# One 32-byte tile fewer ahead of two large operands: a float32r encoder trunk on one core

## The chip, the cores and the metric

The kernel runs on one core of a Trainium2 chip. The metric is the time of one execution on the device in microseconds. Before the change the median of 3 runs is 942.32 us (942.11 to 942.88).

## The reference

Two layers of a bidirectional encoder on x of 256 tokens by 1024 features, float32. Each layer is a half-weighted SwiGLU feed-forward part (FFN), a mixer, and a second FFN part, each behind an RMS norm and added to x. The mixer of layer 0 (even) runs a gated MLP over chunks of 128 tokens beside a differential attention, that of layer 1 (odd) a latent attention beside a grouped attention with axial rotary angles.

```python
for l in range(DEPTH):                                   # 2 layers
    x = x + 0.5 * swiglu(rmsnorm(x, ffn1_norm[l]), ffn1_w_gu[l], ffn1_w_down[l])
    h = rmsnorm(x, ...) @ w_in                           # 1024 -> 2560 (even), 1184 (odd)
    x = x + mixer(h) @ w_out                             # 1024 -> 1024
    x = x + 0.5 * swiglu(rmsnorm(x, ffn2_norm[l]), ffn2_w_gu[l], ffn2_w_down[l])
# swiglu(h): g, u = split(h @ w_gu); (silu(g) * u) @ w_down, width 2816
```

## The kernel before

**Precision.** Each float32 matrix is used as a sum of two float32r parts, hi and lo. A product of two such matrices is hi·hi + lo·hi + hi·lo, three products.

**Weights.** They come from HBM in loads of at most 128 x 2048 floats into four `raw` tiles. `fetch` turns each half (1024 columns) into a `hi` tile (copied, mostly by ScalarE) and a `lo` tile (raw minus hi, by VectorE), in rings of six tiles each.

**Activations.** `xs` (128 x 8 x 2 x 256) holds the normed x: for each of 8 slices of 128 features the 256 tokens of the hi part and behind them the 256 of the lo part. `region` (128 x 11264) holds in an FFN its hidden values `hs` (22 x 2 x 256, in the same form), and in a mixer the head outputs `os_` and the queries and keys.

**Four kinds of matmul stream** follow from this. The stationary operand is written first in the code as `lhsT`, the moving one as `rhs`.

- `wide`, in the FFN: one matmul with a hi weight stationary and 512 columns moving (hi and lo of a slice of `xs` or `hs` at once), then one with the lo weight stationary and the 256 hi columns moving. This is called a pair below. Gate and up take 1408 pairs, with `xs` moving; down takes 682 pairs, with `region` moving.
- `dense` in `out_product` and in the last output tile of the last FFN: three matmuls with weights stationary and 256 columns of `region` moving, 150 such triples.
- `dense` in `block` (the projections into the mixers): here a 128-token part of `xs` is stationary and a row of `hi` or `lo` moves: 512 columns (96 triples), 416 columns (16 triples, of the odd projection `c`) or 256 columns (16 triples, of `k`). `small` does the same with parts of `region` stationary, 12 triples.
- `rms_along`: two matmuls with `onesr` stationary and 256 columns of `acc2` moving, once for each FFN.

In a triple all three matmuls add to the same part of a PSUM bank; in a pair the second adds to half of what the first wrote, and the next pair goes to another bank.

**Order of the work.** `Program` records all instructions, plans an order with its own costs, and emits them in that order; all planned instructions appear in the profile under the line of `emit` that calls them, L285. Dependencies go by the name of a tile and the offsets in it.

**Addresses.** `keep` takes a tile from one pool, and the tiles lie one behind the other in each partition, in the order of the calls, each rounded up to a multiple of 32 bytes. In the program as built, `hi0` begins at byte 76928, which is 128 past a multiple of 256; the other `hi` and `lo` tiles follow in steps of 4096, so all begin at 128 past. `gx` begins at 147968, `ident` at 156416, `ones` at 156928 and `onesr` at 157440, all at multiples of 256. Then comes `warm`, one float in a partition, at 157952, a multiple of 256; it takes 32 bytes. So `region` begins at 157984 and `xs` at 203040, both 32 past a multiple of 256; `rr`, `rb`, `acc`, `acc2` and the tables of the mixers follow, with `rb`, `acc` and `acc2` at 64 past. All slices of `xs` and `hs` that a pair uses begin at multiples of 1024 bytes from there. In the block of 416 columns, a row is 1664 bytes, six and a half times 256, so of the two rows in a `hi` or `lo` tile the first begins at 128 past a multiple of 256 and the second at a multiple of 256.

**Turning tiles.** `sm` is a `Turns` object: 32 tiles of 20 floats, and each call gives a view of the next one, in turn. Small sums and factors of the norms and softmaxes lie in them. They are used in turn by their place in the row of calls, so that call n and call n + 32 share a tile.

**`warm`** is written by one ScalarE activation in the preamble (a Silu over one column of `ones`), ahead of all planned work, and read by nothing.

Of the kernel before, what the change touches and what calls it, by code (L numbers as in the profile page):

```python
# [351 lines left out]
def trunk_kernel(ctx: ExitStack, tc: tile.TileContext, a: dict, out: bass.AP):  # L352
# [20 lines left out]
    def keep(nm, *shape, dt=F32):  # L373
        return sb.tile([P, *shape], dt, name=nm)
# [38 lines left out]
    sm = Turns("sm", 32, 20)  # L413
# [32 lines left out]
    nc.vector.memset(ones, 1.0)  # L446
    onesr = keep("onesr", P, dt=F32R)
    nc.vector.tensor_copy(out=onesr, in_=ones)
    warm = keep("warm", 1)
    nc.scalar.activation(out=warm, in_=ones[:, :1], func=AF.Silu)  # L450
    make_identity(nc, ident)
    with lead(90e3):
# [706 lines left out]
```

## Time and profile before

| | |
|---|---|
| median of 3 runs | 942.32 us |
| profiled execution: its time | 942.35 us |
| its span (first to last instruction) | 940.6 us |
| PE busy | 934.3 us, 5564 matmuls |
| VectorE, ScalarE busy | 724.2 us, 548.2 us |
| chain that ended last | PE 97% |

The span is what lies between the first and the last instruction of the profiled execution; the rest of its time lies around it. PE is the matrix engine, PEld its weight load, which runs beside the matmuls. A matmul's own duration reaches past the start of the next one, since they are pipelined: what a stream costs is read from the distance between starts.

### The profile page before, as it was taken

Reading aid. Unit: us, or ns where it says so; the run is one execution under the profiler, and the core shown is the slowest. Engines: PE = TensorE matmul, PEld = TensorE weight load, DVE = VectorE, ACT = ScalarE, POOL = GpSimd, SP = SyncE. Lnnn points to the kernel's source line nnn. Section 1 sums busy time; section 2 is a strip of 40 time slices with the busy share of each in tenths; the row PEclk is TensorE's granted clock in tenths of the full one; section 3 lists DMA queues with packets and bytes.
Section 4 is the critical chain, followed back from the end, with each engine's and each line's share of the span. In section 5 each row is a group of like instructions: output and inputs, shape, how many; then the busy total and the mean of one; then the engine's idle time right before and its main releaser. Section 6 shows DMA issues by size and latency. Waiting matters only on the chain.

```text
span 940.6 us, 14528 instructions
## 1 busy us (share of the span) xinstructions
PE 934.3 (99%) x5564; PEld 825.5 (88%) x5564; DVE 724.2 (77%) x1326; ACT 548.2 (58%) x938; POOL 27.2 (3%) x57
## 2 busy tenths in 40 slices
PE   9999999999999999999999999999999999999998
PEld 8888888888899888888888888888989988888887
DVE  7998786579989878876588887756888698888652
ACT  7765655446856656655465656544587566565530
POOL 0910000000000000000000000000000000000000
PEclk9999999999999999999999999999999999999999
DMA  8774555553365555555555555554412355555530
GB/s 335 260 268 179 185 194 203 180 179 135 102 212 176 184 192 204 186 179 188 202 184 188 185 198 199 180 184 164 181 54 85 105 186 203 179 185 202 199 110 22
DMA packets 26421, 167.83 MB, mean 178 GB/s; under 512 B 2928, under 2 KB 5104, under 8 KB 7024
## 3 DMA queue, kind: packets, MB, share of 16 engines
q1 hardware_dynamic: 26352, 166.92, 50.4%
q8 instruction: 43, 0.70, 0.3%
q14 instruction: 26, 0.21, 0.1%
HBM read 165.86 MB, written 1.05 MB: 177 GB/s over the span
## 4 chain that ended last, share of the span: by engine, by line
PE 97%; DVE 1%; ACT 1%; DMA 0%; issue 0%; SPq 0%; ACTq 0%
PE bank L285 97%; DVE t L285 0%; ACT t L285 0%; DMA raw<-in_gu 0%; DVE sm L285 0%; ACT hi L285 0%; DVE region L285 0%; DVE lo L285 0%; ACT L285 0%; DVE hi L285 0%; DVE ssg L285 0%; DVE gx L285 0%; SPq L285 0%; DVE ssc L285 0%; DVE rc L285 0%
## 5 line engine op out<-in xcount | busy, mean ns | idle before, releaser
L285 DVE TENSOR_TENSOR lo<-raw,hi 128x1024 fp32r<-128x1024 f32 (+2 forms) x318 | 382.6, 1205 | 161.9 <-ACT hi L285 156.4
L285 ACT ACTIVATE hi<-raw 128x1024 fp32r<-128x1024 f32 (+3 forms) x310 | 322.8, 1044 | 301.1 <-PE bank L285 188.9
L285 PE MATMUL bank<-xs,hi 128*128 128x512 f32 x1408 | 490.7, 393 | 0.3 <-ACT hi L285 0.3
L285 PE MATMUL bank<-xs,lo 128*128 128x256 f32 x1408 | 394.9, 280 | 0.0
L285 PEld LDWEIGHTS bank<-xs,hi 128*128 128x128 f32 x1408 | 265.4, 188 | 58.9 <-ACT hi L285 0.6
L285 PE MATMUL bank<-region,hi 128*128 128x512 f32 (+1 forms) x982 | 291.4, 359 | 0.0
L285 PEld LDWEIGHTS bank<-xs,lo 128*128 128x128 f32 x1408 | 265.3, 188 | 0.7 <-DVE lo L285 0.7
L285 PE MATMUL bank<-region,lo 128*128 128x256 f32 x832 | 232.8, 280 | 0.0
L285 PEld LDWEIGHTS bank<-region,hi 128*128 128x128 f32 x982 | 174.0, 188 | 28.4
L285 PEld LDWEIGHTS bank<-region,lo 128*128 128x128 f32 x832 | 156.3, 188 | 0.0
L285 ACT ACTIVATE t<-bank 128x256 f32<-128x256 f32 (+1 forms) x201 | 76.6, 399 | 39.9 <-PE bank L285 38.8
L285 PE MATMUL bank<-hi,xs 128*128 128x512 f32 (+2 forms) x256 | 78.7, 381 | 0.0
L285 DVE TENSOR_TENSOR t<-bank,t 128x256 f32<-128x256 f32 x176 | 67.3, 420 | 0.7 <-ACT t L285 0.7
L285 DVE TENSOR_TENSOR t<-t,rb 128x512 f32<-128x512 f32 x88 | 60.3, 690 | 1.2
L285 PEld LDWEIGHTS bank<-hi,xs 128*128 128x128 f32 x256 | 47.1, 188 | 8.6
L285 DVE SCALAR_TENSOR_TENSOR gx<-bank,gx 128x256 f32<-128x256 f32 (+1 forms) x71 | 28.3, 451 | 27.2 <-PE bank L285 27.2
L285 PE MATMUL bank<-lo,xs 128*128 128x512 f32 (+2 forms) x128 | 48.0, 375 | 0.0
L285 DVE TENSOR_TENSOR t<-t,t 128x256 f32<-128x256 f32 (+2 forms) x108 | 45.9, 429 | 0.1
L285 ACT ACTIVATE t<-t 128x256 f32<-128x256 f32 (+2 forms) x98 | 39.0, 406 | 3.1 <-DVE t L285 3.0
L285 DVE TENSOR_TENSOR region<-t,region 128x256 fp32r<-128x256 f32 (+2 forms) x92 | 39.2, 431 | 1.1 <-ACT region L285 1.1
L285 ACT ACTIVATE region<-t 128x256 fp32r<-128x256 f32 (+1 forms) x89 | 35.6, 405 | 1.4 <-DVE t L285 1.2
L285 ACT ACTIVATE xs<-gx 128x256 fp32r<-128x256 f32 x48 | 24.0, 499 | 10.8 <-DVE gx L285 10.0
(129 smaller groups left out, 466.8 us busy)
## 6 DMA issues: line engine op xcount, KB each, us to landing
raw<-in_gu SPq DMA_DIRECT2D x86, 1024.0 KB, 4.8
raw<-in_dn SPq DMA_DIRECT2D x44, 1024.0 KB, 4.8
raw<-in_ev_in SPq DMA_DIRECT2D x10, 1024.0 KB, 4.9
raw<-in_ev_out SPq DMA_DIRECT2D x4, 1024.0 KB, 5.1
raw<-in_od_out SPq DMA_DIRECT2D x4, 1024.0 KB, 4.9
raw<-in_gu SPq DMA_DIRECT2D x8, 256.0 KB, 4.5
raw<-in_od_q SPq DMA_DIRECT2D x2, 1024.0 KB, 4.8
raw<-in_od_c SPq DMA_DIRECT2D x2, 832.0 KB, 4.4
```

The costliest lines, as they stand in the source:

```text
L285: r = fn(*map(real, args), **{k: real(v) for k, v in kw.items()})
```

## The change

`warm` is no longer a tile of its own. The activation in the preamble writes to the first turning tile instead, and the first call in the planned work gets the second. Everything that lay behind `warm` lies 32 bytes lower: `region` at 157952 and `xs` at 203008, both multiples of 256; `rb`, `acc` and `acc2` go from 64 to 32 past a multiple of 256. What lies ahead of `warm` stays.

```diff
     onesr = keep("onesr", P, dt=F32R)
     nc.vector.tensor_copy(out=onesr, in_=ones)
-    warm = keep("warm", 1)
+    warm = sm(1)
     nc.scalar.activation(out=warm, in_=ones[:, :1], func=AF.Silu)
     make_identity(nc, ident)
```

## Rows read from the trace of the kernel before

**Rows 1.** The page: span, busy time (share) and instructions, chain that ended last.
```profile
span 940.6 us, 14528 instructions
...
PE 934.3 (99%) x5564; PEld 825.5 (88%) x5564; DVE 724.2 (77%) x1326; ACT 548.2 (58%) x938; POOL 27.2 (3%) x57
...
PE 97%; DVE 1%; ACT 1%; DMA 0%; issue 0%; SPq 0%; ACTq 0%
```

**Rows 2.** Waits of PE, the longest: who for whom, us in total, times, longest.
```profile
PE bank L285 <- DVE ones L446: 1.0, 1, 1.0
```

**Rows 3.** Matmuls by shape: out<-operands, shapes, count, busy us, mean ns, idle.
```profile
L285 PE MATMUL bank<-xs,hi 128*128 128x512 f32 x1408 | 490.7, 393 | 0.3 <-ACT hi L285 0.3
...
L285 PE MATMUL bank<-region,hi 128*128 128x512 f32 x682 | 236.6, 392 | 0.0
...
L285 PE MATMUL bank<-region,hi 128*128 128x256 f32 x300 | 54.8, 284 | 0.0
...
L285 PE MATMUL bank<-hi,xs 128*128 128x512 f32 x192 | 63.7, 401 | 0.0
```

**Rows 4.** Timeline of PE in gate and up: start us, us, instruction; first, last.
```profile
59.86 0.39 PE L285 MATMUL bank<-xs,hi 128*128 128x512 f32 x1
...
90.71 0.39 PE L285 MATMUL bank<-xs,hi 128*128 128x512 f32 x1
```

**Rows 5.** Timeline of PE in down, first and last.
```profile
149.99 0.39 PE L285 MATMUL bank<-region,hi 128*128 128x512 f32 x1
...
180.84 0.39 PE L285 MATMUL bank<-region,hi 128*128 128x512 f32 x1
```

**Rows 6.** Stretches: us, busy and count of each engine, PEclk, DMA share, GB/s.
```profile
59.86:90.71 30.85, 30.85 (x180) 27.16 (x179) 25.68 (x43) 18.80 (x34) 0.00 (x0) 1.00 0.59 211
```

**Rows 7.** Timeline of PE in a block of 512 columns, first and last.
```profile
197.54 0.39 PE L285 MATMUL bank<-lo,xs 128*128 128x512 f32 x1
...
204.54 0.39 PE L285 MATMUL bank<-lo,xs 128*128 128x512 f32 x1
```

**Rows 8.** Timeline of PE in the block of 256 columns, first and last.
```profile
665.32 0.28 PE L285 MATMUL bank<-lo,xs 128*128 128x256 f32 x1
...
667.12 0.29 PE L285 MATMUL bank<-lo,xs 128*128 128x256 f32 x1
```

**Rows 9.** Timeline of PE in the block of 416 columns, first and last.
```profile
672.02 0.35 PE L285 MATMUL bank<-lo,xs 128*128 128x416 f32 x1
...
680.60 0.35 PE L285 MATMUL bank<-lo,xs 128*128 128x416 f32 x1
```

**Rows 10.** Timeline of PE in the even out_product, first and last.
```profile
274.91 0.28 PE L285 MATMUL bank<-region,lo 128*128 128x256 f32 x1
...
283.71 0.28 PE L285 MATMUL bank<-region,lo 128*128 128x256 f32 x1
```

**Rows 11.** Timeline of PE in the odd out_product, first and last.
```profile
742.07 0.28 PE L285 MATMUL bank<-region,lo 128*128 128x256 f32 x1
...
751.68 0.28 PE L285 MATMUL bank<-region,lo 128*128 128x256 f32 x1
```

**Rows 12.** Timeline of PE in rms_along: its two matmuls, and the next.
```profile
294.28 0.40 PE L285 MATMUL bank<-acc,onesr 128*128 128x256 f32 x2
...
294.52 0.39 PE L285 MATMUL bank<-xs,hi 128*128 128x512 f32 x1
```

**Rows 13.** Weight loads by shape: weights stationary, then parts of xs.
```profile
L285 PEld LDWEIGHTS bank<-xs,hi 128*128 128x128 f32 x1408 | 265.4, 188 | 58.9 <-ACT hi L285 0.6
...
L285 PEld LDWEIGHTS bank<-hi,xs 128*128 128x128 f32 x256 | 47.1, 188 | 8.6
```

**Rows 14.** VectorE by shape: writes to region, to acc, to t.
```profile
L285 DVE TENSOR_TENSOR region<-t,region 128x256 fp32r<-128x256 f32 x88 | 36.8, 422 | 1.1 <-ACT region L285 1.1
...
L285 DVE TENSOR_TENSOR acc<-acc,t 128x256 f32<-128x256 f32 x42 | 17.7, 423 | 0.2
...
L285 DVE TENSOR_TENSOR t<-t,t 128x256 f32<-128x256 f32 x96 | 40.1, 422 | 0.1
```

## The prediction

> **What bounds the kernel now.** I read the page first. The matrix engine is busy for 934.3 of 940.6 us, and the chain of work that ended last lies on it for 97% [rows 1]. The list of its waits comes next: the longest is 1.0 us, for the first tile at the start [rows 2]. So neither weights nor evictions hold PE up, and VectorE (77%) and ScalarE (58%) work beside it. The end moves only if the matmuls themselves follow each other at another distance.
>
> The groups by shape say where they are [rows 3]: 1408 pairs of gate and up, 682 pairs of down, then the triples. Their mean durations (393 ns for 512 columns) overlap the next matmul, so the distance has to be read from the timeline. In gate and up 89 pairs start between 59.86 and 90.71 us [rows 4]: 30.85 us / 89 = 346.6 ns a pair. In down 89 pairs take 30.85 us too [rows 5], the same 346.6 ns, though another tile moves. The 2090 pairs are 2090 x 0.3466 = 724 us, three quarters of the span. The granted clock is 1.00 in that stretch, the upper level of 2.4 GHz [rows 6]. A pair moves 768 columns; at one column a cycle that is 320 ns. So 26.6 ns a pair (55.6 us over all) is something other than columns, and this is the only thing that an address could change.
>
> **The change part by part.**
>
> *The tile itself.* The activation that writes `warm` stays, ahead of all planned work: 0. The turning tiles shift by one, for all calls alike, so call n still shares its tile with call n + 32 and with no other. The planned dependencies, and with them the order, are the same. One new pair shares a tile: the activation of the preamble and the 32nd call, whose writer comes long after it: 0. If a semaphore had to be looked at there, it would be on VectorE or ScalarE, with 23% and 42% of their time free [rows 1].
>
> *Moving operands of the pairs.* `xs` and `region` go from 32 past a multiple of 256 bytes to 0 past it. No stream in the trace moves float32r columns that always start at 0 past, so I bound it by the neighbours.
> - 128 past, in `block`: ten triples of 512 columns take 204.54 - 197.54 = 7.00 us [rows 7], 233.3 ns a matmul; five triples of 256 take 1.80 us [rows 8], 120.0 ns. One of each would be 353.3 ns, 6.7 more than an FFN pair.
> - Half at 128 past and half at 0 past, in the block of 416 columns: 15 triples take 680.60 - 672.02 = 8.58 us [rows 9], 190.7 ns a matmul. The straight line between the two points above gives 120.0 + 160 x 113.3 / 256 = 190.8 ns for 416 columns. So the half of the matmuls that begins at a multiple of 256 has not made this stream faster or slower than 128 past would.
> - 32 past, in the two output products: 25 triples of 256 columns take 283.71 - 274.91 = 8.80 us [rows 10], 117.3 ns a matmul; 27 triples take 751.68 - 742.07 = 9.61 us [rows 11], 118.6 ns. The two have the same addresses within 256 bytes and still differ by 1.3 ns: a stream can settle at one of several distances without any change of alignment.
> - 64 past, with `onesr` stationary at 0 past: the two matmuls of `rms_along` take 0.24 us [rows 12], 120 ns each, to some 5 ns.
>
> So 256 columns cost 117 to 120 ns from every start that the trace has. The value I take is 0 for the pairs: the nearest row with starts at multiples of 256, that of 416 columns, lies on the line of the others. The bounds stay wide, because that row mixes two starts and has another stationary operand. Upwards: the pair becomes as slow as the block's streams, 2090 x 6.7 ns = +14.0 us. Downwards: the same difference with the other sign, -14.0 us, since no row shows a pair faster than 346.6 ns.
>
> The Trainium skill, page "TensorE: Matmul & The Clock Gate", section "Back-to-back issue gap", has a rule that a matmul of N columns takes N / 2.4 + 2.5 ns at the upper clock. By it a pair is 324.9 ns, 21.7 less than the rows show, and the trace disagrees with it in each of its float32r streams, at four different starts. If the whole of that surplus came from the misplaced start, the change would give 2090 x 21.7 ns = 45 us and a time near 897 us; I hold that for a rival of 2 in 100.
>
> *The 450 matmuls of 256 columns from `region` (150 triples).* 0, with +0.9 us as the bound above (450 x (120.0 - 118.0)), and -0.9 us below. Their distance may also jump between the 117.3 and 118.6 ns already seen, 0.6 us.
>
> *Stationary operands.* In the blocks, parts of `xs` (in `small`, of `region`) are loaded as weights, now from 0 past. The load's own duration is 188 ns there and 188 ns where `hi` is loaded from 128 past [rows 13]. So 0. The bound below: if the start of the stationary operand is why the blocks are slower than the FFN, 288 matmuls of 512 columns get back 233.3 - 229 = 4 ns, 48 of 416 about 3 ns and 48 of 256 about 2 ns: -1.4 us. (The 229 is the pair's 346.6 less the 117.5 of its 256 columns.) Above: +1.4 us, the same size.
>
> *Element-wise work.* VectorE writes 128 x 256 to `region` (32 past) in 422 ns, to `acc` (64 past) in 423 and to `t` (128 past) in 422 [rows 14]: no start costs anything, and there is slack besides. 0.
>
> Sum: 942.35 us of the profiled execution (span 940.6 and 1.75 around it) + 0 = 942.3 us. That execution lies 0.03 us from the median of the three runs, so no correction is needed.
>
> **The rivals.**
>
> *An aligned start makes the moving reads cheaper.* Something in the 26.6 ns surplus depends on whether a row of columns begins inside a block of 256 bytes: 2048 bytes from 32 past touch nine such blocks, from 0 past eight. For it: the surplus is there in every stream, and all streams of one start throughout lie off the multiple. Against: 416 columns, above. Price: up to 6.7 ns a pair, with half of that as the likeliest, 3.3 x 2090 = -7.0 us: 935.3 us; the whole of it gives 928.3. It decides from 0.9 ns a pair on (1.9 us).
>
> *A start at the multiple behaves like 128 past, not like 32 past.* The FFN pairs have the shortest distance that the trace shows, and it could be 32 past that gives it: a row that begins off the larger boundaries may meet the weight load of the next matmul at another place. The place is each of the 2090 pairs, the price up to 6.7 ns: 942.3 + 14.0 + 0.9 = 957.2 us; with half of it 949.3 us. For it: 416 columns, half of them at 0 past, cost as much as the slower line. Against: the blocks differ in more than the start (three matmuls in a row add to one part of a bank, and `xs` is the stationary side), and 256 columns from 64 past cost no more than from 32. It decides from the same 0.9 ns on, upwards.
>
> *The change doesn't do what it says.* It moves only what lies behind `warm`; if the moved addresses leave every stream as it is, only the stationary side of the blocks can answer, within 1.4 us. That is the forecast's own case, and its time could be 941 to 944.
>
> **How the numbers follow.** A measurement of this kernel can tell about 0.2% (1.9 us) from no change. No change within that: 0.47. Aligned reads are cheaper: 0.33, and the surplus gone altogether 0.02, so faster is 0.35. The start at the multiple is worse: 0.18. The predicted time is that of the likeliest case, 942.3 us, whose own range is 940.5 to 944.2. The range for 8 in 10 takes in most of the first rival (down to 931 us, a little above its whole price) and the smaller prices of the second (up to 948 us); outside are the full gain with the skill's surplus (0.07) and the upper half of the loss (0.10).
>
> **What would show it.** If I am right, the starts of the pairs in gate and up and in down still lie 346.6 ns apart, the 512-column block stays near 233 ns, and the span moves by under 2 us. If the first rival holds, both kinds of pairs shorten alike, since both moving tiles shift, while the 512-column block stays. If only the blocks shorten, it was the stationary side. If the second holds, the pairs come near 350 to 353 ns. A change of order on any engine, or a new wait of PE over 1 us, would show that the reasoning on the turning tiles is wrong.

## The result and the profile after

The change makes the kernel slower: 951.55 us (median of 4, 951.31 to 951.72) against 942.60 (median of 4), ratio 1.0094 with a 95% interval of 1.0082 to 1.0105. The prediction was 942.3 us with 931 to 948 for the range, so the time lies outside it.

The page after, span, busy time and the chain that ended last:

```profile
span 949.8 us, 14528 instructions
...
PE 942.0 (99%) x5564; PEld 829.1 (87%) x5564; DVE 725.1 (76%) x1326; ACT 548.5 (58%) x938; POOL 28.1 (3%) x57
...
PE 95%; DVE 2%; DMA 1%; ACT 1%; SPq 0%; issue 0%; ACTq 0%; DVEq 0%
```

Against [rows 1] the span is 9.2 us longer, PE is busy for 7.7 us more, and the instructions are the same in number and, engine by engine, in the same order. PE still hardly waits: its two longest waits (us in total, times, longest) are

```profile
PE bank L285 <- DVE lo L285: 1.3, 3, 0.9
PE bank L285 <- DVE ones L446: 1.1, 1, 1.1
```

The timeline of PE, first in gate and up, then in down, 90 pairs each (start in us, duration):

```profile
60.05 0.39 PE L285 MATMUL bank<-xs,hi 128*128 128x512 f32 x1
...
91.65 0.39 PE L285 MATMUL bank<-xs,hi 128*128 128x512 f32 x1
...
152.03 0.40 PE L285 MATMUL bank<-region,hi 128*128 128x512 f32 x1
...
183.63 0.40 PE L285 MATMUL bank<-region,hi 128*128 128x512 f32 x1
```

31.60 us / 90 = 351.1 ns a pair in both, where [rows 4, 5] have 346.6. That is 4.4 to 4.5 ns more, times 2090 pairs 9.3 us: the whole of the loss. The granted clock is 1.00 as in [rows 6], and the other engines are about as busy as before. The same 25 us, the kernel before first:

```profile
65.00:90.00 25.00, 25.00 (x146) 22.02 (x145) 20.34 (x34) 15.14 (x28) 0.00 (x0) 1.00 0.53 186
65.00:90.00 25.00, 25.00 (x145) 21.92 (x144) 20.29 (x34) 14.85 (x27) 0.00 (x0) 1.00 0.52 191
```

Looking closer, with the weight loads shown beside the matmuls:

```profile
61.80 0.40 PE L285 MATMUL bank<-xs,hi 128*128 128x512 f32 x1
61.80 0.19 PEld L285 LDWEIGHTS bank<-xs,lo 128*128 128x128 f32 x1
62.04 0.28 PE L285 MATMUL bank<-xs,lo 128*128 128x256 f32 x1
62.04 0.19 PEld L285 LDWEIGHTS bank<-xs,hi 128*128 128x128 f32 x1
62.16 0.39 PE L285 MATMUL bank<-xs,hi 128*128 128x512 f32 x1
...
62.50 0.40 PE L285 MATMUL bank<-xs,hi 128*128 128x512 f32 x1
...
62.86 0.40 PE L285 MATMUL bank<-xs,hi 128*128 128x512 f32 x1
```

Two things are to be seen. The load of the next weights starts together with each matmul, so two operands are read at once: the moving one and the next stationary one. That is so in the kernel before too. And the pairs are uneven now, 0.36, 0.34, 0.36 us; before, each takes 0.34 or 0.35.

The blocks, whose stationary side moved, became a little quicker: ten triples of 512 columns,

```profile
202.16 0.40 PE L285 MATMUL bank<-lo,xs 128*128 128x512 f32 x1
...
209.14 0.39 PE L285 MATMUL bank<-lo,xs 128*128 128x512 f32 x1
```

take 6.98 us, 232.7 ns a matmul against 233.3 [rows 7].

### The profile page after: what moved, and what is told of

It reads as the page before. It is cut to its first block, busy times and chain, and to the rows that moved or that the text cites. A ratio compares the mean times of both kernels' runs of the same rounds, so it can differ in the third digit from the quotient of the medians.

```text
span 949.8 us, 14528 instructions
## 1 busy us (share of the span) xinstructions
PE 942.0 (99%) x5564; PEld 829.1 (87%) x5564; DVE 725.1 (76%) x1326; ACT 548.5 (58%) x938; POOL 28.1 (3%) x57
## 4 chain that ended last, share of the span: by engine, by line
PE 95%; DVE 2%; DMA 1%; ACT 1%; SPq 0%; issue 0%; ACTq 0%; DVEq 0%
PE bank L285 95%; DMA raw<-in_gu 1%; DVE t L285 1%; ACT t L285 0%; DVE lo L285 0%; SPq L285 0%; DVE sm L285 0%; DVE acc L285 0%; DVE region L285 0%; ACT hi L285 0%; DVE hi L285 0%; ACT L285 0%; DVE ssg L285 0%; DVE gx L285 0%; DVE scg L285 0%
## 5 line engine op out<-in xcount | busy, mean ns | idle before, releaser
L285 PE MATMUL bank<-region,hi 128*128 128x512 f32 (+1 forms) x982 | 294.6, 360 | 0.0
```

The costliest lines, as they stand in the source:

```text
L285: r = fn(*map(real, args), **{k: real(v) for k, v in kw.items()})
```

## The experiments

*Distance* below is the start of a moving tile minus that of the weights, in bytes, reduced modulo 256 (modulo 512 in the expectations), and the weights are the hi weights where nothing else is said. Before, it is 32 - 128 = 160; after, 0 - 128 = 128. All edits only place tiles; e10 also makes the planner's bookkeeping finer for two tiles so that its order stays. In the traces of all runs each compute engine's instructions stand in the order of the kernel before. "Pair" is the mean distance between the starts of two pairs in a stage, stalls left out, from the traces. Where no number of runs is given, a time is that of a single run; 13 runs of the kernel before lie between 941.93 and 945.64 us, so the readings of e1 to e10 rest on the pairs and not on the times.

**e1: the turning tile, without the addresses**

```diff
+    keep("pad1", 8)                       # after.py, 32 bytes
     region = keep("region", ARENA, dt=F32R)
```

> The tile of warm is taken from the turning ones as in the change, but an unused tile of 32 bytes stands ahead of region, so that all addresses are those of the kernel before. If the addresses of the moving operands are the cause (theory A: the start within 256 bytes; theory B: the start relative to that of the weights), pairs of 346.7 ns and 942.3 us. If the turning tile or anything else of the change is the cause (theory C), pairs near 351.2 ns and 951.5 us.

943.25 us beside 943.7 of the kernel before; 346.7 ns in both kinds of pairs. Gate and up, 90 pairs in 31.20 us:

```profile
60.07 0.39 PE L285 MATMUL bank<-xs,hi 128*128 128x512 f32 x1
...
91.27 0.39 PE L285 MATMUL bank<-xs,hi 128*128 128x512 f32 x1
```

So the turning tiles cost nothing, and theory C is out.

**e2: one tile at a multiple of 256, the other not**

```diff
     region = keep("region", ARENA, dt=F32R)
+    keep("pad2", 8)                       # after.py
     xs = keep("xs", KT, 2, N, dt=F32R)
```

> The kernel after, with an unused tile of 32 bytes between region and xs: region begins at 0 past a multiple of 256, xs at 32 past. Theories A and B: gate and up (1408 pairs, xs moving) go back to 346.7 ns, down (682 pairs, region moving) stays at 351.2; time 942.3 + 682 x 4.5 ns = 945.4 us. If the state of the whole program decides and not each tile's own address: both kinds of pairs alike, 942 or 951 us.

Gate and up, then down:

```profile
60.17 0.39 PE L285 MATMUL bank<-xs,hi 128*128 128x512 f32 x1
...
91.37 0.39 PE L285 MATMUL bank<-xs,hi 128*128 128x512 f32 x1
...
152.30 0.39 PE L285 MATMUL bank<-region,hi 128*128 128x512 f32 x1
...
183.90 0.39 PE L285 MATMUL bank<-region,hi 128*128 128x512 f32 x1
```

90 pairs in 31.20 us (346.7 ns) and 31.60 us (351.1 ns): each tile's own address decides for its own stream. The time, 948.07 us beside 943.7, is 4.4 us more instead of 3.1. Against the profiled execution before (942.35) it is 5.7 us, and 2.4 of these were lost by the 300th matmul, in the first gate and up, whose pairs are not slower.

**e3: other starts, the weights unmoved**

```diff
+    keep("pad1", 16)                      # after.py
     region = keep("region", ARENA, dt=F32R)
+    keep("pad2", 8)
     xs = keep("xs", KT, 2, N, dt=F32R)
```

> Unused tiles put region at 64 and xs at 96 past a multiple of 256, weights stay at 128. If a start at a multiple of 256 (or of 64) is what costs and every other start is alike: xs at 96 gives 346.7 ns; region at 64 gives 346.7 (multiple of 256 costs) or 351.2 (multiple of 64 costs). If 32 past is a special case, both differ from 346.7 by some ns either way. If a start nearer to that of the weights (128) is better or worse by degrees, xs at 96 lies beyond region at 64.

950.80 us. Down (distance 192) has 353.3 ns. Gate and up (distance 224) has two values in one execution; in the first FFN and in the second, 80 pairs each:

```profile
62.18 0.39 PE L285 MATMUL bank<-xs,hi 128*128 128x512 f32 x1
...
90.45 0.39 PE L285 MATMUL bank<-xs,hi 128*128 128x512 f32 x1
...
322.20 0.39 PE L285 MATMUL bank<-xs,hi 128*128 128x512 f32 x1
...
349.93 0.39 PE L285 MATMUL bank<-xs,hi 128*128 128x512 f32 x1
```

28.27 us are 353.4 ns a pair, 27.73 us are 346.6, at the same addresses. So a start off the multiple of 256 is no safe place either, and the same addresses can give two values, stage by stage. The 350.0 that the expectations below give for 224 is the mean of the two.

**e4: the weights moved too**

```diff
     raws_ = Turns("raw", RAW, SUB)        # before.py
+    keep("pad3", 56)                      # 224 bytes
     his = Turns("hi", RING, PIECE, F32R)
```

> An unused tile of 224 bytes ahead of the hi tiles puts hi and lo at 96 and region and xs at 0 past a multiple of 256: the moving operands begin where they do in the kernel after, but the distance to the weights is that of the kernel before (moving minus stationary = -96). Theory A (the moving start alone): 351.2 ns a pair and 951.5 us. Theory B (the distance between the two starts): 346.7 ns and 942.3 us.

```profile
60.12 0.39 PE L285 MATMUL bank<-xs,hi 128*128 128x512 f32 x1
...
91.32 0.39 PE L285 MATMUL bank<-xs,hi 128*128 128x512 f32 x1
```

346.7 ns in all stages of both kinds, 942.42 us beside 943.7. `region` and `xs` lie at a multiple of 256 and nothing is lost: theory A falls, theory B stands.

**e5, e6, e7: other distances.** The tiles `region32` (e5, e6) and `gx` (all three) change places in the pool.

```diff
+    region32 = keep("region32", ARENA32)  # e5, e6: ahead of raw
     ...
-    gx = keep("gx", NGC + KT * N)         # e5, e6, e7: from ahead of ident ...
+    keep("pad1", ...)                     # 0, 64, 32 bytes
     region = keep("region", ARENA, dt=F32R)
+    keep("pad2", 8)
     xs = keep("xs", KT, 2, N, dt=F32R)
+    gx = keep("gx", NGC + KT * N)         # ... to behind xs
```

> Distance means the start of the moving tile minus that of the weights, in bytes, modulo 512. So far 160 gave pairs of 346.7 ns, 128 of 351.1, 192 of 353.3 and 224 of 350.0. Here region32 and gx change their places in the pool so that region lies at distance 0 and xs at 32 (absolute starts 0 and 32 past a multiple of 256, as in e2). If the distance decides (theory B), both may leave the values of e2 (351.1 for region, 346.7 for xs); if a conflict between the two read streams is worst where they start alike, region is at 353 ns or more. If the absolute start decides after all (theory A), the values of e2 again and 948 us.

> As e5 with 64 bytes more: region at distance 64, xs at 96, absolute starts 64 and 96 as in e3. Theory A: the values of e3 again (353.3 and 350.0 ns, 950.8 us). Theory B: other values; if the effect is symmetric about half of 256 bytes (a distance of 96 is -160), xs at 96 gives 346.7 and region at 64 gives 353.3.

> gx moves behind xs, so that region lies at distance 416 (160 + 256) and xs at 448 (192 + 256). If the distance counts modulo 256 (or a part of it): region 346.7 ns, xs 353.3 ns, time 942.3 + 1408 x 6.6 ns = 951.6 us. If it counts modulo 512 or more, other values.

e5: 346.7 ns for both, 942.99 us beside 942.65, though `region` begins at a multiple of 256 as in e2, where it had 351.1:

```profile
152.08 0.39 PE L285 MATMUL bank<-region,hi 128*128 128x512 f32 x1
...
183.28 0.39 PE L285 MATMUL bank<-region,hi 128*128 128x512 f32 x1
```

Theory A falls again, and so does the guess that like starts are worst. e6: 353.3 at 64 and 350.0 at 96, 951.14 us; the guess of a symmetry fails for 96. e7 has down at 416 (160 + 256) and gate and up at 448 (192 + 256):

```profile
60.23 0.40 PE L285 MATMUL bank<-xs,hi 128*128 128x512 f32 x1
...
92.03 0.40 PE L285 MATMUL bank<-xs,hi 128*128 128x512 f32 x1
...
152.08 0.39 PE L285 MATMUL bank<-region,hi 128*128 128x512 f32 x1
...
183.28 0.39 PE L285 MATMUL bank<-region,hi 128*128 128x512 f32 x1
```

353.3 ns and 346.7 ns, the values of 192 and 160: the distance counts modulo 256 or a part of it. 950.37 us.

**e8: hi and lo weights at different distances, the moving tiles as before**

```diff
     his = Turns("hi", RING, PIECE, F32R)  # after.py
+    keep("pad4", 8)
     los = Turns("lo", RING, PIECE, F32R)
```

> An unused tile of 32 bytes stands between the hi and the lo tiles in place of that of warm: all moving tiles begin as in the kernel before, at distance 160 from the hi weights and 128 from the lo weights. While the 512 hi and lo columns move, a lo weight is loaded; while the 256 columns move, a hi weight. If the load under the 512 columns sets the loss of the kernel after: 351 ns a pair and 951 us. If the load under the 256 columns does: 346.7 ns and 942.3 us. If each has its part: between, near 349 ns.

```profile
60.28 0.39 PE L285 MATMUL bank<-xs,hi 128*128 128x512 f32 x1
...
91.84 0.39 PE L285 MATMUL bank<-xs,hi 128*128 128x512 f32 x1
```

350.7 ns (351.1 in the second layer), 951.79 us beside 942.65. `region` and `xs` begin where they do in the kernel before, and the loss is that of the kernel after: moving 32 bytes on the side of the lo weights is enough. (`region32`, `gx`, `ident`, `ones` and `onesr` move with them; none is an operand of a pair.) It does not follow that the loss lies under the load that moved: the step from the 512 columns to the 256 columns, under which a lo weight is loaded, grew by 2.7 ns in the first layer and the other step by 1.3, while in the kernel after they grew by 1.3 and 3.0.

**e9: the other way round**

```diff
     his = Turns("hi", RING, PIECE, F32R)  # as e6, pad1 32 bytes
+    keep("pad4", 24)                      # 96 bytes
     los = Turns("lo", RING, PIECE, F32R)
```

> An unused tile of 96 bytes between the hi and the lo tiles: region lies at distance 128 from hi and 32 from lo, xs at 160 from hi and 64 from lo (starts past a multiple of 256: region 128, xs 160, hi 0, lo 96). Theory L, the load of the lo weight under the 512 columns sets the pair (e8 speaks for it): region as at 32, 346.7 ns; xs as at 64, 353.3 ns; time 942.3 + 1408 x 6.6 ns = 951.6 us. Theory H, the load of the hi weight under the 256 columns: region as at 128, 351.1, xs as at 160, 346.7; 945.4 us. If both have a part, both kinds of pairs lie between.

949.79 us beside 942.38 (median of 13). Down (128 from hi, 32 from lo): 346.7 ns, as theory L has it. Gate and up (160 and 64): 348.4 in the first FFN, 353.0 to 353.3 in the others; L's 353.3 only in part.

**e10: steps of 16 bytes**

```diff
-    region, xs = keep("region", ARENA, dt=F32R), keep("xs", KT, 2, N, dt=F32R)   # before.py
+    region = keep("region", ARENA + 4, dt=F32R)[:, 4:]
+    xs = view(keep("xs", KT * 2 * N + 4, dt=F32R)[:, 4:], (KT, 2, N))
```

> region and xs begin four floats into their tiles: region at distance 176 (48 past a multiple of 256), xs at 208 (80 past); the order of the instructions is that of the kernel before. If the pair changes by degrees with the distance, region lies between its values at 160 and 192 (346.7 and 353.3), near 350 ns, and xs between 192 and 224 (353.3 and 350.0), near 351.6. If steps of 16 bytes matter by themselves (a start inside a group of 32 bytes), both lie off, and above 353 ns; a value under 346.7 would point to a version faster than both kernels.

950.97 us. Down at 176: 350.0 ns in all stages; gate and up at 208: 350.0 in three stages, 353.3 in one. Nothing below 346.7.

**e11: the whole change kept, the distance another**

```diff
+    keep("pad3", 24)                      # after.py, ahead of hi
     his = Turns("hi", RING, PIECE, F32R)
     ...
+    keep("pad1", 40)                      # 160 bytes
     region = keep("region", ARENA, dt=F32R)
```

> The changed kernel with its region and xs at a multiple of 256, but with unused tiles of 96 bytes ahead of the hi tiles and 160 ahead of region, so that the distance to the weights is 288 (32 modulo 128 and modulo 256). If the distance decides: 346.7 ns in both kinds of pairs, ratio to the kernel before within 0.2% of 1 (942.3 us). If the start at a multiple of 256 costs by itself: 351 ns and 951 us.

```profile
60.01 0.39 PE L285 MATMUL bank<-xs,hi 128*128 128x512 f32 x1
...
91.21 0.39 PE L285 MATMUL bank<-xs,hi 128*128 128x512 f32 x1
...
152.22 0.39 PE L285 MATMUL bank<-region,hi 128*128 128x512 f32 x1
...
183.43 0.39 PE L285 MATMUL bank<-region,hi 128*128 128x512 f32 x1
```

346.7 ns; 941.81 us (10 runs), ratio to the kernel before 0.9994, interval 0.9984 to 1.0003. Warm in a turning tile, both moving tiles at a multiple of 256, and the loss is gone.

**e12: a try below both kernels**

```diff
+    keep("pad4", 56)                      # as e9, 224 bytes; no pad2
```

> The try for a version faster than both: region and xs at distance 256 from hi and 32 from lo. The shortest 512-column step so far stood at 32 from lo (226.7 ns in e9), the shortest 256-column step at 0 from hi (116.7 ns in e5). If the two steps add up freely: pairs of 343.4 ns, 2090 x 3.3 ns = 6.8 us less, ratio 0.993 (935.5 us). If the pair has a floor of 346.7 ns that the weights' distance can only lengthen (every favourable distance so far gave just that): 346.7 ns, ratio within 0.2% of 1.

```profile
60.08 0.39 PE L285 MATMUL bank<-xs,hi 128*128 128x512 f32 x1
...
91.88 0.39 PE L285 MATMUL bank<-xs,hi 128*128 128x512 f32 x1
```

353.3 ns, 954.87 us (4 runs), ratio 1.0131 (1.0114 to 1.0148): the slowest of all. The two steps don't add up, there is no gain to be had this way, and theory L is wrong as a rule: 32 from lo gave 346.7 ns with 128 from hi (e9) and gives 353.3 with 0 from hi.

All placements together, ns a pair; where the stages differ, each value seen:

| from hi, from lo (modulo 256) | pair | kernel |
|---|---|---|
| 160, 160 | 346.7 | before, e1, e2 (xs), e4, e7 (region) |
| 0, 0 | 346.7 | e5 (region) |
| 32, 32 | 346.7 | e5 (xs), e11 |
| 128, 32 | 346.7 | e9 (region) |
| 176, 176 | 350.0 | e10 (region) |
| 96, 96 | 350.0 | e6 (xs) |
| 128, 128 | 351.1 | after, e2 (region) |
| 160, 128 | 350.7, 351.1 | e8 |
| 208, 208 | 350.0, 353.3 | e10 (xs) |
| 160, 64 | 348.4, 353.0, 353.3 | e9 (xs) |
| 224, 224 | 346.7, 353.3 | e3 (xs) |
| 64, 64 | 353.3 | e6 (region) |
| 192, 192 | 353.3 | e3 (region), e7 (xs) |
| 0, 32 | 353.3 | e12 |

## Why the prediction was wrong

**The step that failed** is the one on the moving operands of the pairs, where it says "The value I take is 0 for the pairs: the nearest row with starts at multiples of 256, that of 416 columns, lies on the line of the others." It measured 4.4 ns a pair, 9.3 us over 2090 pairs. The comparison behind it took the start of the moving operand as the thing that a stream's distance depends on, and set streams with other stationary operands beside each other as if these made no difference; that they had another one was noted, but only to widen the bounds. The runs show that the moving start alone decides nothing: at a multiple of 256 the pair takes 351.1 ns in the kernel after and 346.7 in e4, e5 and e11. What counts is where it lies relative to the weights that are loaded meanwhile. The row of 416 columns had its weights 96 or 224 bytes off, and could not speak for an FFN pair that goes to 128. After the change it fell from 190.5 to 188.6 ns a matmul with its moving addresses unchanged, which shows the same thing.

**The rival that came true** is "a start at the multiple behaves like 128 past", by its place and its size: both kinds of pairs, near 351 ns, 949.3 us for half its price and 951.55 measured. It had a chance of 0.18, and the range stopped at 948. Its reason is not what the runs show, though: e4 and e11 have that start without the price. Nearest to them is its aside that a row "may meet the weight load of the next matmul at another place", which set no part of its price. I should have taken the remark in it seriously that the FFN pairs had the shortest distance in the trace: a stream at its best place has more ways to lose than to gain.

**The rival of a cheaper aligned read** falls, with the part that the Trainium skill's rule had in it: in no placement did the pairs of a stage take less than 346.7 ns on the mean. (By that rule a pair is 325.0 ns, not 324.9, and the section gives it for a matmul by itself, while here each matmul has a weight load beside it.)

**The smaller terms held.** Turning tiles: 0, by e1. Elementwise work: the three groups of [rows 14] take 420, 419 and 421 ns after. Stationary side of the blocks: within the 1.4 us stated, by 233.4 to 232.3 ns for 288 matmuls and 1.7 to 2.0 ns for 96 others, some 0.5 us gained. The 450 matmuls of 256 columns: 118.2 to 118.7 ns, 0.2 us lost. The only new wait of PE above 0.3 us is for `lo`: 1.3 us in three places, of which the longest is 0.9.

**Other users of the tiles.** `hi` and `lo` are not only loaded by PE. ScalarE and VectorE write them while pairs run, and these writes keep the same distance to the moving tile, so they could be what the pairs meet. The end of the last FFN speaks against it. After the last write to a weights' tile no instruction of VectorE, ScalarE or GpSimd runs during the 15 pairs that are left, and they still take 5.27 us, 351 ns each:

```profile
931.52 1.22 DVE L285 TENSOR_TENSOR lo<-raw,hi 128x1024 fp32r<-128x1024 f32 x1
...
932.77 0.39 PE L285 MATMUL bank<-region,hi 128*128 128x512 f32 x1
...
938.04 0.39 PE L285 MATMUL bank<-region,hi 128*128 128x256 f32 x2
```

In the kernel before the same 15 pairs take 5.20 us, 346.7 ns each.

**Two reads at once.** The Trainium skill, page "TensorE: Matmul & The Clock Gate", section "Step-by-step: what each phase is for", has it that the matrix engine reads its moving operand and the next weights through two independent ports, so that loading the next weights takes no read bandwidth from the running matmul; its page "SBUF — State Buffer", section "Who interferes with whom", says "PE and ACT never wait on anyone." The measurement does not fit this: with neither instructions nor moving tiles changed, 32 bytes on the side of the lo weights make a pair 4.0 ns longer (e8), so the stream of matmuls does depend on where its next weights lie.

**What stays open.** That the two reads hold each other up is the reading that fits e4, e8, e11 and the last 15 pairs, but no run takes one of the reads away. Which of the placements is good follows no rule that I found: not the distance from lo alone (e9 against e12), and not the distance alone where two values occur (e3). The means 346.7, 350.0 and 353.3 ns are 832, 840 and 848 cycles at 2.4 GHz, but most of the slow ones are means over pairs that differ, in a pattern that repeats every few pairs: 354, 353 and 346 ns in the kernel after, 347 and 359 in gate and up of e12, 353 and 347 in down of e10. At a fast placement the pairs are alike to within a nanosecond or so. What sets these patterns is not shown.

## What to carry to other kernels

A kernel whose matrix engine never waits can still change by 1% when a few bytes are added ahead of its operands, so a comparison of two versions has to look at the distance between matmul starts before it credits or blames the edit. Judge an address by its relation to what is read at the same time, not by its own alignment; and before comparing streams, list everything in which they differ, the other operand first. Where the placement of the large operands is known to be good, keep it: add small tiles behind them, or pad so that the distance to the weights stays.

## What the runs showed of the hardware that was not expected

- The distance between two matmul pairs depends on the addresses of moving tile and weights relative to each other: 346.7 to 353.3 ns over the placements tried, worth up to 12.3 us or 1.3% of this kernel (e12).
- Shifting moving tiles and weights by the same amount changes nothing (e4), and neither does a further 256 bytes of distance (e7).
- The same addresses can give two values of the pair within one execution: 353.4 ns in the first FFN and 346.6 in the second (e3).
- What is good for the FFN is not what is good for the blocks: with `hi` 64 bytes past `xs` a 512-column matmul takes 229 ns (e7) where it took 233.3 before, while the same placement costs the FFN pairs 6.6 ns.
